# A bidirectional Mamba-2 block: gate columns of group 1 into the front, one PSUM ring of five banks in the scan, and three element-wise steps moved

## The chip, the cores and the metric

The kernel runs on one core of one Trainium2 chip. A core has TensorE (PE in the profile, its weight loads PEld), VectorE (DVE), ScalarE (ACT), GpSimd (POOL), SyncE (SP, which here only issues transfers), DMA queues, an on-chip memory called SBUF and the accumulators called PSUM, eight banks of 128 partitions by 512 fp32 numbers. Each engine runs its own instructions in the order in which they were written into its queue, and waits on semaphores for the others. The metric is the device time of one execution, in microseconds (us); lower is better.

## The reference

One layer, 1024 tokens, model width 1024, inner width 2048, 32 heads of 64 in 8 groups of 4, state size 128, chunks of 128 tokens. Everything is fp32.

```
u    = rmsnorm(x)
proj = u @ w_in                       # gate z (2048), x (2048), B and C (8 x 128 each), dt (2 x 32)
xBC  = silu(conv5(x, B, C))           # depthwise, centred
dt   = softplus(dt + bias);  a = -exp(a_log) * dt          # per direction and head
y    = x*d_skip + scan_forward(x*dt, a, B, C) + scan_backward(x*dt, a, B, C)
       # scan, per chunk: (C B^T * exp(segsum a)) x   +   exp(cumsum a) * C state_before
y    = y * silu(z);  y = y * rsqrt(mean over the 256 columns of a group of y^2 + eps)
out  = rmsnorm(x + (y * norm_w) @ w_out)
```

## The kernel before, in words

The program is written as loops over tiles. A scheduler, in which each instruction has a priority by the place where it is written and waits until its buffers are free, then decides the order on each engine. So the code's order and the number of buffers of each pool both move instructions.

**Front.** The eight token tiles of `x` are loaded, normalised, transposed by TensorE and cut into a high and a low fp32r half (`split`, L131 to L134: ScalarE copies, VectorE or GpSimd subtracts), so that three fast matmuls stand for one fp32 product. `z_products` (L137) multiplies one token chunk by a set of 256 gate columns: 8 slices by 3 matmuls, 24 a chunk, 192 a group of gate columns. Group 0's gate columns and the dt columns go this way in the front.

**Pairs.** Sixteen times (eight groups, B and C together and then x) a Strassen form of seven products of 12 matmuls with 512 columns each (`product`, L290; `pair_products`, L314), then the five-tap convolution (`conv`) and the way to DRAM. The weights' sums are made on GpSimd (L274) and split into `wh` and `wl` buffers. After the first pair's products are written, `decays` (L374) makes dt, the decays and their cumulative sums from the dt columns, and stores the rows of cumulative sums in DRAM (`rows_d`). The Strassen sum `t4` is made on GpSimd and split before the first pair.

**Scan.** For each group, `ssd_units` (L559) first builds the seven backward states (`state`, L551: GpSimd makes `xw`, one matmul; `update`, L539, two VectorE operations), and then goes over the eight chunks. One chunk needs, in this order: `mix` (L570), which loads two broadcasts `fb` of the cumulative sums, shifts one by four ScalarE operations (L580), selects by the triangle on VectorE (L582), takes exp on ScalarE (L585), multiplies by C B^T (`pcb`, L588) into `mt` (L590); the state terms `pyo` (L635) and the diagonal term `pyd` (L641) on TensorE; four VectorE operations into `y` (L644), eight ScalarE operations `yo` (L652) and two VectorE adds (L654); the product with the gate on GpSimd (L659); the square with its sum on ScalarE (L661), whose result goes into the unused half of the bank of `pyd`; the norm (L82, L85) and the scaling (L663); and one chunk later a transpose and four stores to `y_d` (`store`, L602).

PSUM in the scan: `pst` gives two banks, in which `pcb` and `pyd` take turns; `psh` gives two, for the states and `pyo`; `ps_ip` has the other four as two tiles of two banks, for gate columns and output units.

**Fills.** TensorE's gaps are filled with other work (`fills`, L769): the gate columns of groups 1 to 7 (`z_stream`, 192 matmuls each, the finished gate stored to DRAM by GpSimd's queue, L526), and then output units of the first half of the inner columns (`out_unit`, L707: 48 matmuls of 512 columns, then the sum with x into `h_d`). `AT` says at which steps of a group a piece is put in; `FIRST` says how many output units are asked for within the scan. What is left comes after the scan, and then the second half of the inner columns (half 1), whose weights `wo1` use the memory that the scan's buffers give up.

## Time and profile before

| | |
|---|---|
| median of 2 runs | 1131.33 us (1130.24 to 1132.42) |
| profiled execution | 1127.91 us, its span 1126.1 us |
| mean granted TensorE clock | 0.925 |
| PE, PEld busy | 977.5 us (87%), 816.6 us (73%) |
| DVE, ACT, POOL busy | 783.6 us (70%), 619.1 us (55%), 377.3 us (34%) |

Busy shares are averages over the whole program. A busy PE is an engine with a matmul under way, and since matmuls overlap and slow down with the clock, 87% is no measure of what is left to win. The stages have different limits, so the rows below are cut by stage: the front up to 153.9 us, the steady pairs to 448.7 us, a transition, the scan from its first diagonal matmul at 482.4 us, and the rest after 1020 us.

### The profile page before, as it was taken

Reading aid. Unit: us, or ns where it says so; the run is one execution under the profiler, and the core shown is the slowest. Engines: PE = TensorE matmul, PEld = TensorE weight load, DVE = VectorE, ACT = ScalarE, POOL = GpSimd, SP = SyncE. Lnnn points to the kernel's source line nnn. Section 1 sums busy time; section 2 is a strip of 40 time slices with the busy share of each in tenths; the row PEclk is TensorE's granted clock in tenths of the full one; section 3 lists DMA queues with packets and bytes.
Section 4 is the critical chain, followed back from the end, with each engine's and each line's share of the span. In section 5 each row is a group of like instructions: output and inputs, shape, how many; then the busy total and the mean of one; then the engine's idle time right before and its main releaser. Section 6 shows DMA issues by size and latency. Waiting matters only on the chain.

```text
span 1126.1 us, 16040 instructions
## 1 busy us (share of the span) xinstructions
PE 977.5 (87%) x5082; PEld 816.6 (73%) x5082; DVE 783.6 (70%) x1487; ACT 619.1 (55%) x1637; POOL 377.3 (34%) x424
## 2 busy tenths in 40 slices
PE   5784799999999999798999989897887897867997
PEld 4773578778778777688888978795665575645786
DVE  5557898788788788677877767867664775754433
ACT  5342455555555546467777757775663573753211
POOL 5349444353353340234333233424212323210000
PEclk9896899999999999899999998997588898968999
DMA  7221135244244227867767776777676766667431
GB/s 234 82 95 37 47 101 161 75 127 135 75 125 138 75 87 233 251 159 171 175 165 173 185 212 163 196 160 197 198 178 202 208 145 164 192 175 246 152 113 56
DMA packets 208212, 170.60 MB, mean 151 GB/s; under 512 B 78512, under 2 KB 177536, under 8 KB 207616
## 3 DMA queue, kind: packets, MB, share of 16 engines
...
HBM read 121.04 MB, written 48.50 MB: 151 GB/s over the span
## 4 chain that ended last, share of the span: by engine, by line
PE 52%; DVE 11%; issue 11%; DMA 9%; ACT 9%; POOL 7%; SPq 1%; POOLq 0%; DVEq 0%; ACTq 0%
PE x L295 12%; PE po L728 11%; PE BC L295 8%; DMA fb<-rows_d 6%; PE pz L146 5%; PE pyd L641 4%; POOL y L659 2%; PE pyo L635 2%; ACT fb L585 2%; ACT fb L580 2%; PE sf L556 1%; ACT yo L652 1%; DMA wo<-in_ssd_w_out_dram 1%; DMA wz<-in_ssd_w_in_dram 1%; PE pcb L588 1%
## 5 line engine op out<-in xcount | busy, mean ns | idle before, releaser
L652 ACT ACTIVATE yo<-pyo,ecs 128x64 f32<-128x64 f32 x448 | 104.2, 311 | 48.9 <-PE pyo L635 27.6
L659 POOL TENSOR_TENSOR y<-y,gt 128x256 f32<-128x256 f32 x64 | 55.3, 864 | 162.5 <-ACT fb L585 59.2
L580 ACT ACTIVATE fb<-fb,cfb 128x128 f32<-128x128 f32 x256 | 83.1, 394 | 48.2 <-DMA fb<-rows_d 43.6
L641 PE MATMUL pyd<-xb,mt 128*128 128x64 f32 x512 | 78.8, 305 | 26.9 <-ACT pyd L661 15.6
L641 PEld LDWEIGHTS pyd<-xb,mt 128*128 128x128 f32 x512 | 74.5, 221 | 36.5 <-ACT pyd L661 25.8
L585 ACT ACTIVATE fb<-fb,cfb 128x128 f32<-128x128 f32 x256 | 82.8, 395 | 20.4 <-DVE fb L582 19.9
L355 DVE SCALAR_TENSOR_TENSOR BC<-BC,prm,BC 128x1022 f32<-128x1022 f32 (+1 forms) x64 | 82.0, 1281 | 6.9 <-ACT BC L349 5.6
L644 DVE SCALAR_TENSOR_TENSOR y<-xb,coef,pyd 128x64 f32<-128x64 f32 x256 | 55.4, 276 | 44.2 <-PE pyd L641 44.0
L355 DVE SCALAR_TENSOR_TENSOR x<-x,prm,x 128x1022 f32<-128x1022 f32 (+1 forms) x64 | 81.8, 1278 | 1.2
L553 POOL TENSOR_TENSOR xwb<-xb,wdt 128x256 f32<-128x256 f32 x56 | 37.8, 684 | 95.0 <-DMA xb<-xb_d 48.7
L553 POOL TENSOR_TENSOR xwf<-xb,wdt 128x256 f32<-128x256 f32 x56 | 37.6, 674 | 88.7 <-PE sf L556 61.3
L582 DVE COPY_PREDICATED fb<-trif,fb 128x512 f32<-128x512 uint32 x64 | 49.8, 779 | 19.6 <-ACT fb L580 19.1
L590 DVE TENSOR_TENSOR mt<-fb,pcb 128x512 f32<-128x512 f32 x64 | 43.6, 683 | 21.9 <-ACT fb L585 21.1
L556 PE MATMUL sb<-xwb,xb 128*128 128x256 f32 x112 | 38.2, 439 | 19.0 <-POOL xwb L553 11.5
L728 PE MATMUL po<-wo1h,yh 128*128 128x512 f32 (+1 forms) x136 | 43.2, 389 | 8.6 <-ACT wo1h L682 7.9
L654 DVE TENSOR_TENSOR y<-y,yo 128x256 f32<-128x256 f32 x112 | 48.9, 437 | 2.4
L728 PE MATMUL po<-wo0h,yh 128*128 128x512 f32 x128 | 47.2, 448 | 3.5 <-ACT yh L132 2.6
L635 PE MATMUL pyo<-pf,ct 128*128 128x256 f32 x112 | 40.1, 443 | 8.7 <-ACT pf L544 4.9
L728 PE MATMUL po<-wo0l,yh 128*128 128x512 f32 x128 | 44.8, 429 | 1.9 <-DVE wo0l L683 1.9
L728 PE MATMUL po<-wo0h,yl 128*128 128x512 f32 x128 | 45.2, 425 | 0.2 <-DVE yl L133 0.2
L661 ACT ACTIVATE pyd<-y 128x256 f32<-128x256 f32 x64 | 24.7, 385 | 37.4 <-POOL y L659 36.9
L588 PE MATMUL pcb<-ct,bt 128*128 128x128 f32 x128 | 30.3, 326 | 16.8 <-ACT pyd L661 13.8
...
## 6 DMA issues: line engine op xcount, KB each, us to landing
fb<-rows_d SPq DMA_DIRECT2D x128, 256.0 KB, 4.7
...
y_d<-yt SPq DMA_DIRECT2D x256, 32.0 KB, 2.4
...
```

Of the source, the lines that this page charges most:

```text
L146: nc.tensor.matmul(pz[:, 0:m], a, b, start=at == 0, stop=at == 3 * NK - 1)
L295: nc.tensor.matmul(ps, a[:, k, :], b[:, k, :], start=fresh and n == 0, stop=n == 11, skip_group_check=True)
L355: nc.vector.scalar_tensor_tensor(out=acc[:, o], in0=ps[:, i], scalar=w(k), in1=acc[:, o], op0=ALU.mult, op1=ALU.add)
L553: nc.gpsimd.tensor_tensor(out=h4(xw), in0=h4(xb[:, 0:CW]), in1=bc4(wdt[:, d, c, g * HG:(g + 1) * HG], HD), op=ALU.mult)
L580: nc.scalar.activation(out=ef[:, h], in_=ef[:, h], func=AF.Identity, bias=cfb[:, 1, c, hsl(g, h)])
L585: nc.scalar.activation(out=ef[:, h], in_=ef[:, h], func=AF.Exp, bias=cfb[:, 0, c, hsl(g, h)])
L635: nc.tensor.matmul(pyo[:, d * CW:(d + 1) * CW], ct[:, tok], st, start=True, stop=True)
L641: nc.tensor.matmul(pyd[:, cs], mt[:, h, :], xb[:, cs], start=True, stop=True)
L644: nc.vector.scalar_tensor_tensor(out=y[:, cs], in0=xb[:, cs], scalar=coef[:, h:h + 1], in1=pyd[:, cs], op0=ALU.mult, op1=ALU.add)
L652: nc.scalar.activation(out=yo[:, cs], in_=pyo[:, d * CW + h * HD:d * CW + (h + 1) * HD], func=AF.Copy, scale=ecs[:, d, c, hsl(g, h)])
L659: nc.gpsimd.tensor_tensor(out=y, in0=y, in1=gt, op=ALU.mult)
L728: nc.tensor.matmul(pos[i], l_, r_[:, cols[i]], start=k == 0 and a == 0, stop=k == NO - 1 and a == 2)
```

## The change

Eight things are different.

1. PSUM. The two-bank pools now live only until the pairs end. In the scan there are three single banks for fills (`ps_z`) and one ring of five (`ps_h`), which `pcb`, `pyo`, `pyd` and the states share. After the scan, half 1 has five banks (`ps_o`). Gate columns are made two chunks at a time in one bank, and an output unit takes two single banks, so its sum with x becomes two operations.
2. The gate columns of group 1 (192 matmuls) are made in the front, and `decays` is written right behind them and ahead of the first pair.
3. Token tiles 2 and 6 of `x` are loaded into a tile of the weights' pool; the pool of high halves has 9 buffers, not 10.
4. Finished gates are stored through SP's queue in pieces of two chunks, not through GpSimd's in pieces of four.
5. The shift of the exponents is one GpSimd add on 128x512 instead of four ScalarE operations on 128x128.
6. The product of y and the gate is on VectorE, not on GpSimd.
7. The squares of y go to a tile in SBUF, not to the bank of `pyd`. `xw` has three buffers, not two.
8. `FIRST` is 7, `AT` has a 5 in place of a 6, the first four output weights are loaded while the last gate columns are made, and all eight weights of half 1 are asked for at once.

```diff
+    def z_group(g, w, bank, room, nxt=None):
+        for c0 in range(0, NC, 2):
+            gt = room(f"gate{g}_{c0}", (P, 2, CW))
+            pz = bank(f"pz{g}_{c0}").rearrange("p (i n) -> p i n", i=2)
+            for c in (c0, c0 + 1):
+                z_products(pz[:, c % 2], c, w, CW)
+                if c % 2:
+                    gate_of(gt, pz)
+                    nc.sync.dma_start(out=gate_d[g, :, c0:c0 + 2], in_=gt)
+                if c == NC // 2 and nxt is not None:
+                    nxt()
+                yield
...
-    WBUFS = {"h": 10, "l": 12}
+    WBUFS = {"h": 9, "l": 12}
...
-        xt = big(f"xt{t}")
+        if t == 2:
+            xts["pair"] = wpb.tile([P, 2, DM], F32, tag="raw", name="xt26")
+        xt = xts["pair"][:, t // 4] if t in (2, 6) else big(f"xt{t}")
...
+    for _ in z_group(1, load_z(1, wpb, (P, 4, 512)), pst, lambda n, sh: small("h", n, sh)):
+        pass
+    rows_v = decays()
...
-        if n == 0:
-            rows_v = decays()
...
-    ps_h = ctx.enter_context(tc.tile_pool(name="ps_h", bufs=2, space=PSUM))
+    ps_z = ctx.enter_context(tc.tile_pool(name="ps_z", bufs=3, space=PSUM))
+    ps_h = main.enter_context(tc.tile_pool(name="ps_h", bufs=5, space=PSUM))
...
-                        nc.gpsimd.dma_start(out=gate_d[g, :, c0:c0 + 4], in_=gt)
...
-        xw = sp.tile([P, CW], F32, tag="xw", name="xw" + name, bufs=2)
+        xw = sp.tile([P, CW], F32, tag="xw", name="xw" + name, bufs=3)
...
-            for h in range(HG):
-                nc.scalar.activation(out=ef[:, h], in_=ef[:, h], func=AF.Identity,
-                                     bias=cfb[:, 1, c, hsl(g, h)])
+            nc.gpsimd.tensor_tensor(out=ef, in0=ef, in1=bc4(cfb[:, 1, c, g * HG:(g + 1) * HG], P),
+                                    op=ALU.add)
...
-            pcb = pst(f"pcb{g}_{c}")
+            pcb = psh(f"pcb{g}_{c}")
...
-            pyd = pst(f"pyd{g}_{c}")
+            pyd = psh(f"pyd{g}_{c}")
...
-            nc.gpsimd.tensor_tensor(out=y, in0=y, in1=gt, op=ALU.mult)
+            nc.vector.tensor_tensor(out=y, in0=y, in1=gt, op=ALU.mult)
...
-            nc.scalar.activation(out=pyd[:, CW:2 * CW], in_=y, func=AF.Square, accum_out=ss)
+            junk = sp.tile([P, CW], F32, tag="junk", name=f"sq{g}_{c}", bufs=1)
+            nc.scalar.activation(out=junk, in_=y, func=AF.Square, accum_out=ss)
...
-            po = ps_ip.tile([P, DM], F32, tag="ip", name=f"po{half}{t}")
-            pos = [po[:, cs] for cs in cols]
+            pos = [obank(half)(f"po{half}{t}_{i}") for i in range(2)]
...
-            nc.vector.tensor_tensor(out=h, in0=po, in1=h, op=ALU.add)
+            for cs, pi in zip(cols, pos):
+                nc.vector.tensor_tensor(out=h[:, cs], in0=pi, in1=h[:, cs], op=ALU.add)
...
-    FIRST = 5
+    FIRST = 7
...
-        yield from z_stream(wz1)
-        for k in range(NO):
+        w = {2: wz2}
...
+        for g in range(2, NG):
+            yield from z_group(g, w.pop(g), psz, big, more(g))
+        for k in range(4, NO):
...
-    AT = (2, 6, 8, 9, 10, 11, 12, 13, 14, 15)
+    AT = (2, 5, 8, 9, 10, 11, 12, 13, 14, 15)
...
-        for _ in range(3):
+        for _ in range(NO):
```

The diff moves most instructions of the scan, and three places show how. The first is TensorE's order in group 4 of the scan, from the diagonal matmuls of chunk 1 on; `sf` is a forward state, `pz7` a gate fill of group 7. Before:

```order
L556 MATMUL sf4_1_7436<-xwf4_1_7434,xb4_1_7225 128x256
L588 MATMUL pcb4_2_7401<-ct4_7149,bt4_7148 128x128
L641 MATMUL pyd4_1_7412<-xb4_1_7225,mt4_1_7305 128x64 x4
L635 MATMUL pyo4_2_7501<-pf4_1_7438,ct4_7149 128x256
L635 MATMUL pyo4_2_7501<-pb4_2_7222,ct4_7149 128x256
L556 MATMUL sf4_2_7528<-xwf4_2_7526,xb4_2_7216 128x256
L146 MATMUL pz7_0_7643<-wz7_0h_7345,b11h_114 128x256
L146 MATMUL pz7_0_7643<-wz7_0l_7346,b11h_114 128x256
```

After the change, from chunk 0's state on:

```order
L565 MATMUL sf4_0_7572<-xwf4_0_7570,xb4_0_7507 128x256
L596 MATMUL pcb4_2_7623<-ct4_7376,bt4_7375 128x128
L643 MATMUL pyo4_1_7631<-pf4_0_7574,ct4_7376 128x256
L643 MATMUL pyo4_1_7631<-pb4_1_7458,ct4_7376 128x256
L649 MATMUL pyd4_1_7634<-xb4_1_7452,mt4_1_7546 128x64 x4
L565 MATMUL sf4_1_7658<-xwf4_1_7656,xb4_1_7452 128x256
L596 MATMUL pcb4_3_7715<-ct4_7376,bt4_7375 128x128
L643 MATMUL pyo4_2_7723<-pf4_1_7660,ct4_7376 128x256
L643 MATMUL pyo4_2_7723<-pb4_2_7449,ct4_7376 128x256
L649 MATMUL pyd4_2_7726<-xb4_2_7443,mt4_2_7625 128x64 x4
L565 MATMUL sf4_2_7750<-xwf4_2_7748,xb4_2_7443 128x256
```

What moved: `pcb` of chunk c+2 now stands ahead of `pyo` and `pyd` of chunk c+1, the forward state stands behind `pyd`, and no gate fill stands between these chunks; before, the next diagonal matmul in this order (chunk 2) stands behind 45 fill matmuls.

The second place is SP's queue in group 0 of the scan, chunks 2 to 4; `fb` are the broadcasts for `mix`, `gt` the gate that a chunk needs, `gate_d` is written by a store. Before:

```order
L442 DMA wz4_0_5315<-in_ssd_w_in_dram 128x4x256
L576 DMA fb0_2_3919<-rows_d_76 128x512 x2
L576 DMA fb0_3_4011<-rows_d_76 128x512 x2
L568 DMA xb1_7_4547<-xb_d_78 128x384
L626 DMA gt0_2_4009<-gate_d_80 128x256
L610 DMA y_d_77<-yt0_0_3979 32x8x32 x4
L576 DMA fb0_4_4106<-rows_d_76 128x512
L626 DMA gt0_3_4104<-gate_d_80 128x256
L576 DMA fb0_4_4106<-rows_d_76 128x512
```

After the change:

```order
L572 DMA ct1_4799<-bc_d_79 128x1024
L585 DMA fb0_2_4158<-rows_d_76 128x512 x2
L163 DMA gate_d_80<-gate2_0_3840 128x512
L163 DMA gate_d_80<-gate2_2_3893 128x512
L585 DMA fb0_3_4250<-rows_d_76 128x512 x2
L577 DMA xb1_7_4802<-xb_d_78 128x384
L634 DMA gt0_2_4248<-gate_d_80 128x256
L585 DMA fb0_4_4343<-rows_d_76 128x512
L163 DMA gate_d_80<-gate2_4_4005 128x512
L585 DMA fb0_4_4343<-rows_d_76 128x512
L577 DMA xb1_6_4804<-xb_d_78 128x384
L618 DMA y_d_77<-yt0_0_4216 32x8x32 x4
```

What moved: stores of gates now stand in SP's queue ahead of loads of `fb` and `gt` that the scan needs next. Between the first and the last chunk of the scan there are 24 of them; before, this queue had none and GpSimd's had all.

The third place is TensorE's order at the end of the scan, the last chunk of group 7; `po07` is output unit 7 of the first half, `po10` unit 0 of half 1. Before:

```order
L635 MATMUL pyo7_7_10187<-pf7_6_10168,ct7_9586 128x256
L588 MATMUL pcb7_7_10131<-ct7_9586,bt7_9585 128x128
L641 MATMUL pyd7_6_10142<-xb7_6_9591,mt7_6_10065 128x64 x4
L641 MATMUL pyd7_7_10189<-xb7_7_9589,mt7_7_10133 128x64 x4
L728 MATMUL po07_10389<-wo0h0_8298,yh070_10341 128x512 x2
L728 MATMUL po07_10389<-wo0l0_8299,yh070_10341 128x512 x2
```

After the change:

```order
L649 MATMUL pyd7_6_10226<-xb7_6_9692,mt7_6_10151 128x64 x4
L565 MATMUL sf7_6_10250<-xwf7_6_10248,xb7_6_9692 128x256
L643 MATMUL pyo7_7_10272<-pf7_6_10252,ct7_9687 128x256
L649 MATMUL pyd7_7_10274<-xb7_7_9690,mt7_7_10217 128x64 x4
L740 MATMUL po10_0_10428<-wo1h0_10385,yh100_10350 128x512
L740 MATMUL po10_1_10429<-wo1h0_10385,yh100_10350 128x512
```

What moved: the 48 matmuls of output unit 7 (six rows of two for each of four weights pairs) no longer stand between the last diagonal matmul and half 1; they are now within the scan.

## Rows read from the trace of the kernel before

**Rows 1.** Stretches: window, length, busy (instructions) PE, PEld, DVE, ACT, POOL; PEclk, DMA, GB/s.
```profile
0.00:74.90 74.90, 51.89 (x302) 47.77 (x302) 37.64 (x64) 31.11 (x59) 28.64 (x38) 0.93 0.47 150
74.90:153.90 79.00, 55.26 (x211) 41.38 (x212) 64.80 (x61) 32.43 (x52) 54.30 (x37) 0.81 0.19 54
153.90:448.70 294.80, 291.51 (x1330) 234.74 (x1328) 242.65 (x228) 166.00 (x253) 114.13 (x89) 1.00 0.39 120
482.40:1020.00 537.60, 463.65 (x2670) 395.57 (x2668) 374.07 (x1054) 350.24 (x1207) 168.20 (x244) 0.90 0.70 180
1020.00:1126.10 106.10, 91.12 (x408) 74.02 (x408) 42.16 (x55) 26.36 (x41) 4.38 (x8) 0.95 0.43 140
```

**Rows 2.** Gate matmuls, timeline of PE: start and length in us, engine, line.
```profile
554.37 0.28 PE L146 MATMUL pz<-wz_2h,b21h 128*128 128x256 f32 x1
555.67 0.28 PE L146 MATMUL pz<-wz_3h,b21l 128*128 128x256 f32 x1
```

**Rows 3.** The decays' first matmul, timeline of PE; idle before it in brackets.
```profile
126.76 0.77 PE L415 MATMUL pa<-dt,trif 128*128 128x256 f32 x1 [7.39 <-DVE dt L412]
```

**Rows 4.** Stretches of scan groups 1 and 5, and the sum over eight groups.
```profile
539.90:597.20 57.30, 54.16 (x395) 50.30 (x394) 45.90 (x132) 42.10 (x148) 23.04 (x33) 1.00 0.73 181
788.10:886.40 98.30, 78.33 (x287) 58.47 (x286) 60.46 (x146) 53.78 (x170) 21.67 (x31) 0.76 0.71 195
sum 537.60, PE 463.65 PEld 395.57 DVE 374.07 ACT 350.24 POOL 168.20; mean PE 57.96 PEld 49.45 DVE 46.76 ACT 43.78 POOL 21.03
```

**Rows 5.** Waits in the scan: engine, tile, line, releaser; total us, times, longest.
```profile
POOL xwf L553 <- PE sf L556: 61.3, 30, 4.7
ACT fb L580 <- DMA fb<-rows_d: 37.1, 24, 6.4
POOL gate_d L526 <- DVE gate L151: 17.3, 10, 5.3
PE pyd L641 <- ACT pyd L661: 15.6, 14, 4.1
PE pcb L588 <- ACT pyd L661: 13.8, 16, 3.2
```

**Rows 6.** Costliest groups of the page: busy us, mean ns, idle before.
```profile
L580 ACT ACTIVATE fb<-fb,cfb 128x128 f32<-128x128 f32 x256 | 83.1, 394 | 48.2 <-DMA fb<-rows_d 43.6
L659 POOL TENSOR_TENSOR y<-y,gt 128x256 f32<-128x256 f32 x64 | 55.3, 864 | 162.5 <-ACT fb L585 59.2
L654 DVE TENSOR_TENSOR y<-y,yo 128x256 f32<-128x256 f32 x112 | 48.9, 437 | 2.4
L661 ACT ACTIVATE pyd<-y 128x256 f32<-128x256 f32 x64 | 24.7, 385 | 37.4 <-POOL y L659 36.9
```

**Rows 7.** Line 663's instructions: min/median/max ns, first and last start.
```profile
L663 ACT ACTIVATE y<-y,y_7r x8: 507/509/510, 535.8 to 1010.7; 128x256 f32<-128x256 f32 x8
```

**Rows 8.** GpSimd and VectorE on 128x512 tiles, timeline of the front.
```profile
108.64 1.72 POOL L274 TENSOR_TENSOR wx0s<-wx0r 128x512 f32<-128x512 f32 x1
109.15 1.76 DVE L133 TENSOR_TENSOR wx0s2l<-wx0s,wx0s2h 128x512 fp32r<-128x512 f32 x1
...
126.53 0.68 DVE L133 TENSOR_TENSOR wBC1s2l<-wBC1s,wBC1s2h 128x512 fp32r<-128x512 f32 x1
...
141.77 1.29 POOL L274 TENSOR_TENSOR wx1s<-wx1r 128x512 f32<-128x512 f32 x1
```

**Rows 9.** From the last chunk to the first matmul of half 1, timeline.
```profile
1010.70 0.51 ACT L663 ACTIVATE y<-y,y_7r 128x256 f32<-128x256 f32 x1 [0.85 <-POOL y_7r L85]
...
1019.24 1.23 DVE L733 TENSOR_TENSOR h<-po,h 128x1024 f32<-128x1024 f32 x1 [4.82 <-PE po L728]
1020.38 0.43 DVE L606 STREAM_TRANSPOSE yt<-y 128x256 f32<-128x256 f32 x1
...
1024.15 2.19 ACT L682 ACTIVATE wo1h<-wo,prm 128x1024 fp32r<-128x1024 f32 x2 [6.34 <-DMA y_d<-yt]
...
1025.40 1.19 PE L728 MATMUL po<-wo1h,yh 128*128 128x512 f32 x2 [6.19 <-ACT wo1h L682]
```

More of the change, by code (lines that the diff above doesn't have):

```diff
@@ L56 @@
     dram = ctx.enter_context(tc.tile_pool(name="dram", bufs=1, space=bass.MemoryType.DRAM))
-    ps_ip = ctx.enter_context(tc.tile_pool(name="ps_ip", bufs=2, space=PSUM))
-    ps_g = ctx.enter_context(tc.tile_pool(name="ps_g", bufs=2, space=PSUM))
+    first = ExitStack()
+    ps_g = first.enter_context(tc.tile_pool(name="ps_g", bufs=2, space=PSUM))
+    ps_ip = first.enter_context(tc.tile_pool(name="ps_ip", bufs=2, space=PSUM))
     def pst(name):
@@ L94 @@
     dec = main.enter_context(tc.tile_pool(name="dec", bufs=1, side="right"))
-    first = ExitStack()
     ps_x = first.enter_context(tc.tile_pool(name="ps_x", bufs=1, space=PSUM))
@@ L199, in load_z0, with load_z @@
         return at
+    def load_z(g, pool, shape):
+        at = []
+        for i in range(2):
+            raw = pool.tile([P, 4, CW], F32, tag="raw", name=f"wz{g}_{i}", padded_shape=shape)
+            nc.sync.dma_start(out=raw, in_=w_in[:, 4 * i:4 * i + 4, g * CW:(g + 1) * CW])
+            for j in range(2):
+                hi, lo = (wtile(p, f"wz{g}_{2 * i + j}{p}", (P, 2, CW)) for p in "hl")
+                split(raw[:, 2 * j:2 * j + 2], hi, lo)
+                at += [(hi[:, n], lo[:, n]) for n in range(2)]
+        return at
     def to_cm(src, dst, tok, name):
@@ L705, in out_prep, with obank @@
         return h, yh, yl
+    ps_o = []
+    def obank(half):
+        return psz if half == 0 else lambda name: ps_o[0].tile([P, 512], F32, tag="o", name=name)
     def out_unit(half, t, wo, prep, nxt):
@@ L716, in out_unit @@
             steps = [(k, a, i) for i in range(3) for k, a in ka]
-            pos = [pst(f"po{i}")[:, 0:cs.stop - cs.start] for i, cs in enumerate(cols)]
+            pos = [obank(half)(f"po{i}")[:, 0:cs.stop - cs.start] for i, cs in enumerate(cols)]
         else:
-            po = ps_ip.tile([P, DM], F32, tag="ip", name=f"po{half}{t}")
-            pos = [po[:, cs] for cs in cols]
+            pos = [obank(half)(f"po{half}{t}_{i}") for i in range(2)]
             steps = [(k, a, i) for k, a in ka for i in range(2)]
@@ L732, in out_unit @@
         if half == 0:
-            nc.vector.tensor_tensor(out=h, in0=po, in1=h, op=ALU.add)
+            for cs, pi in zip(cols, pos):
+                nc.vector.tensor_tensor(out=h[:, cs], in0=pi, in1=h[:, cs], op=ALU.add)
             nc.sync.dma_start(out=h_d[tok, :], in_=h)
             return nprep
-        parts = list(zip(cols, pos)) if last else [(slice(0, DM), po)]
+        parts = list(zip(cols, pos))
         ss = ops.tile([P, 3], F32, tag="ss", name=f"oss{t}")
@@ L765, in finish, with more, do @@
                 return end.value
-    FIRST = 5
+    FIRST = 7
     wo1, preps = [], []
     def fills():
-        yield from z_stream(wz1)
-        for k in range(NO):
+        w = {2: wz2}
+        def more(g):
+            def do():
+                if g < NG - 1:
+                    w[g + 1] = load_z(g + 1, wp2, (P, 4, CW))
+                else:
+                    for k in range(4):
+                        if k % 2 == 0:
+                            tiles = wo_tiles(up, 0, k // 2)
+                        wo1.append(load_wo(tiles, 0, k))
+            return do
+        for g in range(2, NG):
+            yield from z_group(g, w.pop(g), psz, big, more(g))
+        for k in range(4, NO):
             if k % 2 == 0:
@@ L810 @@
     prep = preps[-1]
+    ps_o.append(ctx.enter_context(tc.tile_pool(name="ps_o", bufs=5, space=PSUM)))
     for t in range(NC):
```

30 lines of the change are left out of this document (5 added, 25 removed).

## The prediction

> **What bounds the kernel now.** I read the granted clock and engine shares first, then the span cut by stage [rows 1], then the scan by group [rows 4] and its waits [rows 5]; durations come from the page [rows 6] and single stretches of the timeline.
>
> The cut by stage shows where time can still be found. In the steady pairs TensorE is busy 291.5 of 294.8 us at clock 1.00: nothing is left there. Two stages are not like that. From 74.9 to 153.9 us TensorE is busy 55.3 of 79.0 us, so 23.7 us are idle, and its clock is 0.81, between the chip's two levels of 1.2 and 2.4 GHz. In the scan it is busy 463.7 of 537.6 us at 0.90, VectorE 374.1, ScalarE 350.2, GpSimd 168.2. No engine is full in the scan, so its length is set by waits of one engine for another.
>
> Which waits, the scan's list tells [rows 5]. The matmuls of `pyd` and `pcb` wait 15.6 and 13.8 us for the square of L661, since that square lies in the bank of `pyd` and both tiles share two banks: a chunk's bank comes free only after y, its adds, the gate product on GpSimd and the square. GpSimd waits 61.3 us for a forward state before it may overwrite one of two `xw`. ScalarE waits 37.1 us, once 6.4 us, for a broadcast `fb`. The groups differ: group 1 takes 57.3 us with TensorE busy 54.2 at clock 1.00, group 5 takes 98.3 us at 0.76 [rows 4].
>
> **The change part by part.** The sum is made against the profiled execution, 1127.91 us, which lies 3.4 us under the median of 1131.33; 3.4 us are added at the end.
>
> *x tiles.* More room lets two of eight loads start earlier. TensorE idles 23.0 of the first 74.9 us [rows 1], but the first loads and the splits hold it too, and no row parts them. Bounds 0 to -6 us (a quarter of that idle time); I take -3, the middle.
>
> *Gate columns of group 1 and the decays in the front.* Twelve gate matmuls start within 1.30 us [rows 2], so one takes 0.118 us and 192 take 22.7 us. They stand where TensorE now has 23.7 us idle, of which one wait of 7.39 us is the decays' first matmul, called for by VectorE after pair 0 has begun [rows 3]. In the change the decays' VectorE work runs under the 192 matmuls, and pair 0 starts later by these but without that wait. What stays uncovered is the wait for `t4`, whose sums run on GpSimd (busy 54.3 of 79.0 us there). If it all fits, the cost is 0; if nothing does, +22.7. Since the room is just the size of the work, but the clock of 0.81 leaves some more, I take 0, and keep -3 to +23. Leaving the scan, the same 192 matmuls give TensorE 22.7 us there, counted below.
>
> *Nine buffers of high halves.* A pair keeps seven live, so two are left for the next pair instead of three. The stage has 3.3 us of TensorE idle time now. Taken as 0; bounds 0 to +8 (0.6 us in each of some 14 pairs).
>
> *The shift on GpSimd.* ScalarE loses 256 operations, 83.1 us, nearly all inside the scan's stretch [rows 6]. GpSimd gains 64 adds on 128x512; such an add took it 1.29 us alone and 1.72 beside VectorE [rows 8], 83 to 110 us in all. It loses 55.3 us of gate products [rows 6]. GpSimd in the scan: 168.2 - 55.3 + 83 to 110 = 196 to 223 us, below half of the stage, so it is not the bound by its sum. The latency of a chunk's shift, four times 394 ns = 1.58 us before, is about the same.
>
> *The gate product on VectorE.* The nearest row is the add of the same shape, 437 ns [rows 6]: 64 x 0.437 = 28.0 us more on VectorE. A chunk's chain loses 0.43 us (864 - 437 ns) and one crossing between engines.
>
> *Squares to SBUF.* A ScalarE pass on the same 128x256 from SBUF to SBUF takes 508 ns [rows 7], to PSUM 385 [rows 6]: 64 x 0.12 = 7.9 us more on ScalarE, which has 350.2 - 83 + 8 = 275 us of work left in the scan. Hidden: ScalarE then has over 200 us free, and nobody waits for the bank any more. The Trainium skill, "ScalarE: Activation LUTs", section "Step-by-step: what each stage is for", says that ScalarE writes to PSUM faster than to SBUF; both rows here agree, and by it this step is a loss, which is worth it only if the bank was the wait.
>
> *Five banks in a ring.* A chunk takes four banks (`pcb`, `pyo`, `pyd`, `sf`). With five, a bank is asked for again five takes later, and it comes free after y, after `yo` or after the state update, not after the square. The 29.4 us of TensorE's waits for L661 go, and so does most of the 61.3 us of GpSimd, which was not on TensorE's path by itself (third `xw`).
>
> *What the scan then takes.* Two floors. VectorE: 374.1 + 28.0 = 402. To it comes contention: VectorE operations from SBUF are stretched while GpSimd adds (1.76 us against 0.68 [rows 8], 1.08 us more). GpSimd's adds in the scan rise by 28 to 55 us net; the adds of L654 (48.9 us) and the gate product (28) are a fifth of VectorE's 402 us, and with the selects of L582 I take 30% of its time to be operations from SBUF, so I put 12 us: 414, or 51.8 us a group. TensorE: group 1 has 257 gate matmuls in its order, 30.3 of 54.2 us, which leaves 24 us of a group's own matmuls; 8 x 24 and the fills make 400: six groups of gate columns at 22.7 us, less 14 that run before the scan, and the 384 matmuls of eight output units at 91.12/408 = 0.223 us [rows 1], 208 in all. VectorE is the larger. What a group takes above VectorE's work now is 57.3 - 45.9 = 11.4 us in an undisturbed group [rows 4], 7.7 if the 29.4 us of bank waits, 3.7 a group, come off in full. So 8 x (51.8 + 7.7 to 11.4) = 476 to 505, and I take 488, **-50** us. It comes mostly from the slow groups 4 to 7, where TensorE's clock fell after waits. Bounds: -95 (all waits gone but 3 us a group: 8 x 54.8 = 438, rounded up for the dearer transition) and the rivals below.
>
> *Gate stores on SP.* 14 issues leave GpSimd's queue, where one had waited 1.7 us on average for its data (17.3 us over 10 [rows 5]); 24 come onto SP's in the scan, each half as large. Behind a waiting store stand the loads of `fb` and `gt`. A load is issued a chunk ahead, so at 1.7 us each I take 0; at worst see the second rival.
>
> *End of the scan.* Now, after the last scaling ends at 1011.2, TensorE does output unit 7, VectorE adds it at 1019.24 for 1.23 us, and only then comes the last transpose at 1020.38; its stores land, `wo1h` starts at 1024.15 and half 1 at 1025.40 [rows 9]. With unit 7 inside the scan the transpose can follow the scaling: 1011.3 + 0.4, then the same 3.3 and 1.25 us, so about 1016.3 instead of 1025.4: **-9**. Bounds -10 to -4. The 48 matmuls, 10.7 us, are in the fills above.
>
> *Output units in single banks, weights of half 1 all at once:* the same matmuls and one more VectorE start each; 0, bounds -3 to +3, hidden behind 48 matmuls a unit.
>
> Sum: 1127.9 - 3 + 0 + 0 - 50 - 9 = 1065.9, and with 3.4 **1069 us**.
>
> **The rivals.** A measurement of this kernel can tell about 2%, 23 us, from no change: faster means under 1109, slower over 1154.
>
> *VectorE held up by GpSimd.* Each of the 64 large adds might meet a VectorE operation from SBUF and stretch it by the full 1.08 us: 69 us, VectorE 374 + 28 + 69 = 471, 58.9 a group, and with 7.7 to 11.4 on top 533 to 562 us of scan, middle 548: 1127.9 - 12 + 10 + 3.4 = 1129. For it: the doubled row, and that the change puts the gate product, an operation with two SBUF operands, beside the adds. Against it: most of VectorE's work in the scan reads PSUM or one operand. The Trainium skill, "SBUF — State Buffer", section "Who interferes with whom", has the rule: VectorE's second port pair is GpSimd's, under an exclusive lock. The stretched row agrees; by that rule part 5 of the change speaks against part 6. The chance of this rival is 13%.
>
> *Slower: SP's head of line.* A gate store that waits for its gate holds `fb` and `gt` behind it; `fb` is what starts the next `mix`. If each of the 24 costs the scan the longest wait that GpSimd's stores had, 5.3 us [rows 5], that is 127 us: 1069 + 127 = 1196. It decides once a store costs more than (1154 - 1069)/24 = 3.5 us. For it: `fb` already makes ScalarE wait up to 6.4 us, and two buffers give little lead. Against: mean waits were 1.7 us. Chance 10%.
>
> *The front does not hide group 1.* The 192 matmuls lengthen the front by 22.7 us: 1092. For it: the wait for `t4` is on GpSimd and may move behind them. Chance 12%.
>
> *The ring does not free.* Five takes back from the next `pyd` stands `pyo`, freed by eight ScalarE operations of `yo`; if that comes as late as the square did, the chunk's pace stays and the scan wins only the 22.7 us that left it, less the 10.7 of unit 7: 1127.9 - 3 - 12 - 9 + 3.4 = 1107. Chance 8%.
>
> **The numbers.** The forecast has 57% (range 1035 to 1105). The range must hold 80%: forecast, front and ring cases, and a part of the first rival: 1030 to 1118. Left out are SP's case, most of the first rival, and a little below. Faster: nearly all of the forecast, the front's 12% and half of the ring's 8%, about 72%; same: 18%; slower: 10%.
>
> **What would show it.** In the profile after: no wait of `pyd` or `pcb` for the square, and none in its place; the scan's stretch at 475 to 505 us with VectorE at 400 to 420; groups 4 to 7 near 60 us and a clock near 1.00; GpSimd's adds at 1.3 to 1.7 us; pair 1 starting at about 154 us; half 1 within 10 us of the last diagonal matmul. Wrong would be: VectorE's two-operand operations at twice their time, `fb` waits above 37 us with a store ahead of them on SP, a new wait of TensorE for `yo`, or pair 1 at 175.

## The result, and the profile after

The change made the kernel slower: 1160.11 us (1159.33 to 1160.89) against 1131.33, ratio 1.0254 [1.0203, 1.0306]. The forecast was 1069, the range 1030 to 1118.

The cut by stage of the kernel after, with the columns of [rows 1], cut where pair 2 is first copied (pairs counted from 0; the prediction's signs call it pair 1) and where the scan's first diagonal matmul starts:

```profile
0.00:74.90 74.90, 51.23 (x306) 46.91 (x306) 37.98 (x65) 31.66 (x60) 29.81 (x38) 0.93 0.40 136
74.90:163.10 88.20, 75.54 (x400) 63.71 (x400) 59.96 (x68) 36.02 (x58) 49.72 (x36) 0.90 0.32 91
163.10:457.00 293.90, 280.77 (x1279) 225.32 (x1278) 236.95 (x214) 157.63 (x240) 126.37 (x89) 1.00 0.36 106
...
505.30:1046.00 540.70, 443.21 (x2485) 382.76 (x2483) 388.39 (x1128) 274.34 (x959) 167.47 (x226) 0.86 0.66 175
1046.00:1159.20 113.20, 91.38 (x408) 74.57 (x408) 44.81 (x72) 30.09 (x60) 4.95 (x9) 0.89 0.41 132
```

The front takes 163.1 us instead of 153.9. TensorE does fill its idle time there (75.5 of 88.2 us), but the stage is longer by 9.2. In the scan VectorE is at 388 us, near the forecast 402, ScalarE at 274, where 275 was forecast. The engines' sums are near the forecast or below it; the stage is not.

A table tells where the time lies, worked out from the start of each chunk's first diagonal matmul and from the first copies of pairs 2 and 15. "Chunks" are the seven steps within each group, "transitions" the seven steps from a group's last diagonal matmul to the next group's first.

| us | front | pairs 2 to 15 | to the scan | chunks | transitions | rest |
|---|---|---|---|---|---|---|
| before | 153.9 | 276.1 | 52.5 | 400.6 | 122.1 | 120.9 |
| after | 163.1 | 287.7 | 54.5 | 355.5 | 178.4 | 120.0 |
| difference | +9.2 | +11.6 | +2.0 | -45.1 | +56.3 | -0.9 |

The chunks did become shorter, by 45 us, 28.5 of them in group 5 alone, whose seven steps fell from 67.5 to 39.0 us (in the other groups they took 44.8 to 50.3 before). Nearly everything else went the other way. Groups 4 to 6, which were to come near 60 us at a clock near 1.00, take 80.0, 70.0 and 71.4 us at 0.78, 0.91 and 0.85; before, they took 64.4, 98.3 and 71.5. The waits of the scan after, as in [rows 5]:

```profile
POOL xwf L562 <- PE sf L565: 80.3, 26, 6.4
POOL fb L588 <- DMA fb<-rows_d: 52.3, 21, 5.1
PE pyd L649 <- DVE mt L598: 44.0, 17, 18.3
DVE fb L590 <- POOL fb L588: 43.8, 30, 5.7
```

No wait of `pyd` or `pcb` for the square is in the list: this step did what it said. In its place `pyd` waits 44.0 us for `mt`, once 18.3, and `mt` for a chain that begins with GpSimd waiting for `fb`. The costliest groups, as in [rows 6]:

```profile
L588 POOL TENSOR_TENSOR fb<-fb,cfb 128x512 f32<-128x512 f32 x61 | 65.4, 1072 | 77.0 <-DMA fb<-rows_d 52.3 <-ACT fb L593 10.1 <-issue 4.3
L662 DVE TENSOR_TENSOR y<-y,yo 128x256 f32<-128x256 f32 x112 | 50.3, 449 | 2.4 <-ACT yo L660 1.6
L667 DVE TENSOR_TENSOR y<-y,gt 128x256 f32<-128x256 f32 x63 | 27.4, 434 | 0.4
L670 ACT ACTIVATE sq<-y 128x256 f32<-128x256 f32 x63 | 26.6, 422 | 25.7 <-DVE y L667 25.4
```

The shift takes GpSimd 1.07 us, less than the 1.29 taken from [rows 8]. VectorE's operations from SBUF take 434 and 449 ns on average, against 437 in [rows 6]. These means hide that few of them meet the shift. Of the 112 adds ten overlap it, and these take 697 ns on average; the 91 that meet no GpSimd instruction over 0.3 us take 414, none more than 426. One that does, by the timeline (start, length, engine, line, operation):

```profile
788.99 1.04 POOL L588 TENSOR_TENSOR fb<-fb,cfb 128x512 f32<-128x512 f32 x1 [2.01 <-DMA fb<-rows_d]
789.32 0.99 DVE L662 TENSOR_TENSOR y<-y,yo 128x256 f32<-128x256 f32 x1
```

With four products of the gate that overlap it (664 ns against 417), this adds up to about 4 us in the whole scan.

The growth of the transitions is uneven: 5.2, 18.5, 20.7 and 11.0 us in the transitions from groups 0, 1, 3 and 4, and 1.2 us or less in the three others. The one that grew most is shown here. First its stretch before (group 3 to 4) and after, columns as in [rows 1]:

```profile
713.00:723.70 10.70, 9.51 (x66) 8.45 (x67) 8.77 (x26) 5.65 (x18) 5.69 (x9) 1.00 0.63 149
```

```profile
746.50:777.90 31.40, 10.19 (x56) 8.44 (x55) 17.06 (x34) 9.77 (x21) 10.13 (x14) 0.69 0.69 192
```

TensorE is busy 9.5 of 10.7 us before and 10.2 of 31.4 after, at a clock of 0.69. The timeline of the transition before, around the last diagonal matmul of group 3 (start, length, engine, line, operation; SPq is SP's queue):

```profile
710.61 0.86 SPq L576 DMA_DIRECT2D fb<-rows_d  x2
712.99 1.07 PE L641 MATMUL pyd<-xb,mt 128*128 128x64 f32 x8 [0.30 <-DVE y_6m L82]
713.83 1.80 SPq L610 DMA_DIRECT2D y_d<-yt  x4
715.74 0.40 SPq L568 DMA_DIRECT2D xb<-xb_d  x1
716.25 0.36 SPq L626 DMA_DIRECT2D gt<-gate_d  x1
```

The last `xb` of the next group is issued 2.8 us after that matmul; the next group's first `fb` was issued 2.4 us before it. The same place after the change (last diagonal matmul at 746.54):

```profile
756.36 1.80 SPq L618 DMA_DIRECT2D y_d<-yt  x4
758.20 0.92 SPq L688 DMA_DIRECT2D wo<-in_ssd_w_out_dram  x2
759.97 1.83 SPq L618 DMA_DIRECT2D y_d<-yt  x4
762.00 2.41 ACT L691 ACTIVATE wo0h<-wo,prm 128x1024 fp32r<-128x1024 f32 x2 [1.46 <-DMA wo<-in_ssd_w_out_dram]
764.49 1.61 SPq L688 DMA_DIRECT2D wo<-in_ssd_w_out_dram  x2
766.16 0.42 SPq L577 DMA_DIRECT2D xb<-xb_d  x1
766.63 0.90 SPq L585 DMA_DIRECT2D fb<-rows_d  x2
...
771.32 2.73 POOL L562 TENSOR_TENSOR xwf<-xb,wdt 128x256 f32<-128x256 f32 x3 [14.88 <-DMA xb<-xb_d]
774.02 1.03 POOL L588 TENSOR_TENSOR fb<-fb,cfb 128x512 f32<-128x512 f32 x1
...
777.90 0.69 PE L649 MATMUL pyd<-xb,mt 128*128 128x64 f32 x2 [18.33 <-DVE mt L598]
```

SP issues stores of y, two output weights, stores of y again, and then waits until a raw weight has been read (ScalarE starts on it at 762.00) before it can issue the next two at 764.49. Only behind these come `xb` at 766.16 and `fb` at 766.63, 20 us after the last diagonal matmul. GpSimd idles 14.9 us for `xb`, and the first diagonal matmul of group 4 waits 18.3 us. By the start times of the loads, the mean over the seven transitions is: last `xb` 5.4 us after the last diagonal matmul before and 13.3 after, first `fb` 4.2 and 13.7, first diagonal matmul 17.4 and 25.5. On average the transition grew by what the loads came later.

The end of the scan, timeline, as in [rows 9]; first the last diagonal matmul before, then the kernel after:

```profile
1005.16 1.94 PE L641 MATMUL pyd<-xb,mt 128*128 128x64 f32 x8 [4.40 <-DVE y_6m L82]
```

```profile
1039.19 1.97 PE L649 MATMUL pyd<-xb,mt 128*128 128x64 f32 x8 [0.59 <-DVE mt L598]
...
1044.32 0.45 DVE L614 STREAM_TRANSPOSE yt<-y 128x256 f32<-128x256 f32 x1 [0.55 <-DMA y_d<-yt]
...
1049.66 0.45 DVE L614 STREAM_TRANSPOSE yt<-y 128x256 f32<-128x256 f32 x1 [0.32 <-DMA y_d<-yt]
1050.07 0.51 ACT L672 ACTIVATE y<-y,y_7r 128x256 f32<-128x256 f32 x1 [1.18 <-POOL y_7r L86]
...
1053.25 0.45 DVE L614 STREAM_TRANSPOSE yt<-y 128x256 f32<-128x256 f32 x1 [0.38 <-DMA y_d<-yt]
1053.72 1.79 SPq L618 DMA_DIRECT2D y_d<-yt  x4
...
1058.80 2.19 ACT L691 ACTIVATE wo1h<-wo,prm 128x1024 fp32r<-128x1024 f32 x2 [1.28 <-DMA y_d<-yt]
1060.05 1.62 PE L740 MATMUL po<-wo1h,yh 128*128 128x512 f32 x3 [18.90 <-ACT wo1h L691]
```

Output unit 7 is gone from this place, and yet half 1 starts 20.9 us after the last diagonal matmul starts, as before (1005.16 to 1025.40, 20.2 us). Four transposes into the one buffer `yt` (at 1039.38 and the three shown) stand behind it, each after the stores of the one before; before there were three (at 1006.00, 1010.07 and, behind unit 7, 1020.38). No run gave `yt` a second buffer, so that this backlog is the wait is read from the timeline alone.

### The profile page after: what moved, and what is told of

Its sections match the earlier page's. It is cut to its first block, busy times and chain, and to the rows that moved or that the text cites. A ratio compares the mean times of both kernels' runs of the same rounds, so it can differ in the third digit from the quotient of the medians.

```text
span 1159.2 us, 15961 instructions
## 1 busy us (share of the span) xinstructions
PE 977.0 (84%) x5082; PEld 822.8 (71%) x5082; DVE 803.1 (69%) x1587; ACT 548.6 (47%) x1409; POOL 389.6 (34%) x410
## 4 chain that ended last, share of the span: by engine, by line
PE 52%; DVE 13%; DMA 12%; issue 8%; ACT 6%; POOL 6%; SPq 3%; POOLq 0%; DVEq 0%; ACTq 0%
PE po L740 12%; PE pz L146 11%; PE x L323 9%; PE BC L323 8%; DMA fb<-rows_d 6%; PE pyd L649 4%; PE pyo L643 2%; DVE x L383 2%; POOL fb L588 2%; PE sf L565 2%; DMA xb<-xb_d 2%; DMA wo<-in_ssd_w_out_dram 2%; SPq L618 1%; ACT fb L593 1%; DMA y_d<-yt 1%
## 5 line engine op out<-in xcount | busy, mean ns | idle before, releaser
L649 PEld LDWEIGHTS pyd<-xb,mt 128*128 128x128 f32 x512 | 77.0, 225 | 63.0 <-DVE mt L598 58.0
L593 ACT ACTIVATE fb<-fb,cfb 128x128 f32<-128x128 f32 x256 | 83.0, 392 | 77.1 <-DVE fb L590 70.6
L588 POOL TENSOR_TENSOR fb<-fb,cfb 128x512 f32<-128x512 f32 x64 | 68.5, 1071 | 88.8 <-DMA fb<-rows_d 64.2
L562 POOL TENSOR_TENSOR xwf<-xb,wdt 128x256 f32<-128x256 f32 x56 | 36.7, 665 | 105.0 <-PE sf L565 80.3
L565 PE MATMUL sb<-xwb,xb 128*128 128x256 f32 x112 | 40.6, 480 | 25.1 <-POOL xwb L562 17.4
L662 DVE TENSOR_TENSOR y<-y,yo 128x256 f32<-128x256 f32 x112 | 50.3, 449 | 2.4 <-ACT yo L660 1.6
L565 PEld LDWEIGHTS sb<-xwb,xb 128*128 128x128 f32 x112 | 22.4, 231 | 35.6 <-POOL xwb L562 29.8
L740 PE MATMUL po<-wo1l,yh 128*128 128x512 f32 (+1 forms) x136 | 43.3, 386 | 0.7 <-DVE wo1l L692 0.7
L151 DVE SCALAR_TENSOR_TENSOR gate<-gate,pz 128x512 f32<-128x512 f32 x32 | 21.8, 682 | 31.7 <-ACT gate L150 31.7
```

What stands on the lines that cost most here:

```text
L562: nc.gpsimd.tensor_tensor(out=h4(xw), in0=h4(xb[:, 0:CW]), in1=bc4(wdt[:, d, c, g * HG:(g + 1) * HG], HD), op=ALU.mult)
L565: nc.tensor.matmul(ps[:, 0:CW], xb[:, CW:CW + P], xw, start=True, stop=True)
L588: nc.gpsimd.tensor_tensor(out=ef, in0=ef, in1=bc4(cfb[:, 1, c, g * HG:(g + 1) * HG], P), op=ALU.add)
L593: nc.scalar.activation(out=ef[:, h], in_=ef[:, h], func=AF.Exp, bias=cfb[:, 0, c, hsl(g, h)])
L649: nc.tensor.matmul(pyd[:, cs], mt[:, h, :], xb[:, cs], start=True, stop=True)
L740: nc.tensor.matmul(pos[i], l_, r_[:, cols[i]], start=k == 0 and a == 0, stop=k == NO - 1 and a == 2)
```

## The experiments

Runs on "the change" start from the kernel after, those on "before" from the kernel before; `comb1` and what follows it are described where they come. All times are medians, ratios are to the kernel before on the same chip.

**One buffer less** (`b_h9`, on before).

```diff
-    WBUFS = {"h": 10, "l": 12}
+    WBUFS = {"h": 9, "l": 12}
```

> The kernel before with 9 instead of 10 buffers for high halves, nothing else. In the profile of the change the steady pairs (from the first copy of pair 2 to that of pair 15) take 287.7 us against 276.0. Theory A, the lost buffer costs this: the stretch becomes 285 to 290 us here and the total 1140 to 1146. Rival B, the cost comes from the decays and the gate columns of group 1 being written ahead of the pairs: stretch 276 to 278, total 1130 to 1134.

1138.05 us, 1.0084 [1.0057, 1.0111]; pairs 290.0 us. The buffer alone costs the pairs 13.9 us, and the rival is out: with ten buffers and the gate columns in the front the pairs take 275.8 us (`c_z1_front`, below). TensorE's one long idle time in a group's pairs is the same in the change and here:

```profile
215.80 1.06 PE L397 MATMUL x0t_1p<-ident,x 128*128 128x128 f32 x8 [1.86 <-DVE x L387]
```

```profile
206.87 1.66 PE L369 MATMUL x0t_1p<-ident,x 128*128 128x128 f32 x8 [1.85 <-DVE x L359]
```

With nine buffers the transposes of x stand in TensorE's order 1.9 us before VectorE has their operand, once in each group; in the kernel before, this wait is 0.8 us once and else under 0.4. The rest of the run also shows how far the split of the scan can move by itself: its chunks are 384.6 and its transitions 142.1, 16 us less and 20 more than before, though no line of the scan differs.

**Single parts of the change undone** (`a_shift_act`: ScalarE's shift of before; `a_gate_pool`: `nc.gpsimd.dma_start` for the gate; `a_sched`: part 8 undone but for the weights of half 1; `a_z1_scan`: part 2 undone).

> The change with the exponents' shift back on ScalarE. Theory Q: in the change the diagonal matmuls wait 44 us for mt, whose chain runs through GpSimd's queue, where the shift stands behind the tiny power operations that wait for the norm; back on ScalarE the scan (533.9 us from the first to the last diagonal matmul) loses 20 to 40 us, total 1120 to 1140. Rival S: the chain is late because SP's queue issues fb late (gate stores, y stores and output weights ahead of it); then total 1155 to 1165, and the wait of ScalarE for fb comes back.

> The change with the gate stores back on GpSimd's queue (pieces of two chunks). Rival S (SP's head of line by gate stores): the scan loses 20 us or more, total under 1140. Theory Q: GpSimd's queue gets 24 more waits, total 1158 to 1170.

> The change with FIRST 5, AT with its 6, and all eight output weights of half 0 loaded after the last gate columns, as before. Theory W: the 18.3 us wait at the start of group 4 of the scan comes from two output weights ahead of xb and fb in SP's queue, waiting for a raw buffer; it goes, and the part from group 3's last diagonal matmul to group 5's first (111.3 us) falls to about 95; total 1140 to 1150. If the schedule only moves this wait to the next group: 1155 to 1165. The 48 matmuls of unit 7 return to the end of the scan in part: +5 to +9 there.

> The change with the gate columns of group 1 made in the scan again and the decays behind pair 0 again; the nine buffers stay. Front (to the first copy of pair 2) 163.1 us in the change, 153.9 before. Theory F: the 192 matmuls were hidden only in part, so the front falls to about 154 (-9) and the scan's fills grow by 22.7 us; if the scan has idle time for them (TensorE idles 93 of 534 us there) the scan grows by 5 or less and the total is 1150 to 1157; if the scan is paced by its fills, it grows by 15 to 23 and the total is 1165 to 1173.

| on the change | us | ratio | front | chunks | transitions | rest |
|---|---|---|---|---|---|---|
| shift on ScalarE | 1148.50 | 1.0188 [1.0135, 1.0241] | 162.6 | 370.5 | 158.1 | 115.2 |
| gate stores by GpSimd | 1147.02 | 1.0164 [1.0117, 1.0210] | 166.7 | 346.8 | 167.9 | 121.4 |
| old schedule | 1161.22 | 1.0296 [1.0238, 1.0354] | 163.7 | 370.7 | 157.7 | 124.3 |
| group 1 in the scan | 1154.19 | 1.0217 [1.0168, 1.0266] | 152.9 | 364.7 | 167.2 | 117.6 |

By medians the shift and the gate stores cost 12 and 13 us, by ratios 7 and 10, between what their two theories had said. All four intervals overlap with that of the change, so these runs alone are weak, and three of the parts are put to `comb1` below. The schedule is a wash: the 31.4 us transition falls to 21.1, but the weights now come inside group 4, whose chunks rise from 54.8 to 70.1. With group 1 back in the scan the front is 10.2 us shorter and the scan, which has 22.7 us more of TensorE's work, is not longer (532.0 against 533.9): TensorE's work does not set the scan's time.

**The square's place and the ring alone** (`b_sq_yo`, on before; `ring_only`, whose PSUM pools are the change's).

```diff
-            nc.scalar.activation(out=pyd[:, CW:2 * CW], in_=y, func=AF.Square, accum_out=ss)
+            nc.scalar.activation(out=yo, in_=y, func=AF.Square, accum_out=ss)
```

> The kernel before with one operand changed: the squares go to the dead tile yo in SBUF, not to the bank of pyd. Theory R (the step of the prediction): the 29 us of waits of pyd and pcb for the square go, and the scan (522.7 us from first to last diagonal matmul) falls by 15 to 30 us; total 1100 to 1115. Theory C (the wait only changes its name, since a chunk is paced by the chain fb, shift, select, exp, mt): same within 5 us, 1126 to 1136, with pyd waiting for mt instead.

> The kernel before with the PSUM layout of the change (three banks for fills, a ring of five for the scan, half 1 in five, gates stored in pieces of two chunks through GpSimd's queue) and the squares in SBUF; ten buffers, shift on ScalarE, gate product on GpSimd, FIRST 5, xw 2, group 1 in the scan. Theory R: scan below 500 us, total 1095 to 1110. Theory C: 1125 to 1138.

1123.61 us, 0.9962 [0.9934, 0.9990], and 1115.71 us, 0.9879 [0.9840, 0.9917]; chunks and transitions 370.4 and 143.2, 368.7 and 140.6. Both theories were too sure. Waits of the scan of `b_sq_yo`:

```profile
DVE y L644 <- PE pyd L641: 21.9, 33, 1.9
PE pyd L641 <- DVE pcb L594: 19.1, 17, 5.7
PE pyd L641 <- DVE mt L590: 13.5, 3, 5.6
```

The waits for the square (29.4 us in [rows 5]) are gone. In their place stand 32.6 us for C B^T's diagonal and `mt`, of which 6.5 were there before and 5.6 lie ahead of the first diagonal matmul: about 20 us are new, and the scan is 9.0 us shorter (513.7 against 522.7).

**A version that is faster** (`comb1`): `ring_only`, but with the gate product on VectorE and what it lacked of part 8 (it already asks for all weights of half 1 at once). That is the change without parts 2, 3, 4 (pieces of two chunks stay, on GpSimd's queue) and 5, the squares in the dead tile `yo`, and two `xw`.

> As ring_only, but with the gate product on VectorE and the schedule of the change (FIRST 7, AT 5, four output weights early, weights of half 1 at once). Theory R: 9 us below ring_only at the end of the scan. Theory C: the output weights ahead of xb and fb cost 10 to 20 us at the start of a group, as in the change; total not below ring_only.

1103.11 us, 0.9759 [0.9710, 0.9809]. Three of the parts left out were then put back alone (`c_gate_sp`, `c_shift_pool`, `c_z1_front`), and the gate product put back on GpSimd (`c_ygt_pool`). Nine buffers were run alone only on the kernel before; the third `xw`, the squares' own tile and the tiles of x were not run alone.

> comb1 (1103 us) with the exponents' shift on GpSimd, nothing else. Theory Q (the shift in GpSimd's in-order queue is late, the mt chain with it): scan 8 to 15 us longer, total 1110 to 1120, ScalarE waiting for the select (L588) more than the 32.6 us of comb1 at that place. Rival: on a kernel without gate stores in SP's queue the shift costs nothing, total 1098 to 1108, and the cost in the change was SP's.

> comb1 with the gate stores in SP's queue, nothing else. Theory S (SP's head of line): 28 stores hold loads of fb, xb and gt behind them, scan 10 to 20 us longer, total 1113 to 1123. Rival: the 52.6 us that GpSimd waits for gates in comb1 weigh as much, total 1095 to 1108.

> comb1 with the gate product on GpSimd. If the gate product on VectorE is what makes comb1 12 us faster than ring_only: 1112 to 1118. If the schedule (FIRST 7, weights early) does: 1100 to 1106.

> comb1 with the gate columns of group 1 and the decays ahead of the pairs, ten buffers kept. Theory F: the front grows by 7 to 10 us (its idle time is no room, since t4 and the weights' sums come later too), the pairs stay at 276, the scan gives back at most 5 though its fills lose 22.7 us, since waits pace it; total 1105 to 1113. Rival: with ten buffers the front hides it and the scan gains 10 to 20, total 1083 to 1095.

| on comb1 | us | ratio | front | chunks | transitions | rest |
|---|---|---|---|---|---|---|
| comb1 | 1103.11 | 0.9759 [0.9710, 0.9809] | 155.8 | 357.0 | 138.9 | 116.5 |
| shift on GpSimd | 1140.63 | 1.0078 [1.0048, 1.0109] | 156.0 | 366.0 | 158.2 | 122.2 |
| gate stores by SP | 1128.60 | 0.9964 [0.9939, 0.9988] | 154.6 | 370.0 | 149.3 | 118.7 |
| group 1 in the front | 1128.82 | 0.9983 [0.9959, 1.0008] | 167.6 | 362.3 | 147.4 | 116.6 |
| gate product on GpSimd | 1115.24 | 0.9858 [0.9810, 0.9907] | 153.0 | 367.8 | 141.1 | 116.2 |

The chips of the runs differ, so the costs are taken from the ratios, times 1131 us: 36 us for the shift, 23 for the gate stores, 25 for group 1, each with intervals apart from that of `comb1` and more than was expected. The gate product on VectorE is worth 11 us, and the rest of part 8 nothing: `c_ygt_pool` differs from `ring_only` by it alone, 1115.24 and 1115.71. The waits of `comb1` and of the run with GpSimd's shift:

```profile
ACT fb L586 <- DMA fb<-rows_d: 38.7, 25, 7.0
DVE fb L588 <- ACT fb L586: 32.6, 26, 8.9
PE pyd L647 <- DVE mt L596: 23.2, 16, 6.0
ACT fb L591 <- DVE fb L588: 6.8, 10, 1.3
```

```profile
POOL fb L585 <- DMA fb<-rows_d: 60.0, 26, 4.2
DVE fb L587 <- POOL fb L585: 58.4, 35, 8.7
ACT fb L590 <- DVE fb L587: 50.2, 30, 9.2
PE pyd L646 <- DVE mt L595: 31.1, 21, 6.2
```

With the shift on ScalarE, exp waits 6.8 us for the select and the select 32.6 for the shift; with it on GpSimd these are 50.2 and 58.4. Yet the shift does not come late: from the issue of a chunk's second `fb` load to the end of its select the mean of the 64 chunks is 8.6 us in `comb1` and 8.1 with GpSimd's shift. What comes later is y and the next group. From a chunk's first diagonal matmul to the last of its stores it is 17.7 us instead of 15.1, and the last `xb` of the next group is issued 10.8 us after the last diagonal matmul instead of 6.7. What ties this to the shift is not shown.

**Taking loads out of SP's queue, and opening the loop over `fb`.** `a_fb_act` and `c_fb_act` issue `fb` by `nc.scalar.dma_start`, `a_xb_pool` and `c_ef4_xb` issue `xb` by `nc.gpsimd.dma_start`. `a_ef4` and `c_ef4`:

```diff
-            fb = sp.tile([P, 2, HG, P], F32, tag="fb", name=f"fb{g}_{c}")
+            fb = [sp.tile([P, HG, P], F32, tag=f"fb{d}", name=f"fb{d}{g}_{c}", bufs=(2, 4)[d])
+                  for d in range(2)]
...
-            mt = sp.tile([P, HG, P], F32, tag="mt", name=f"mt{g}_{c}")
+            mt = ef
```

> The change with the loads of fb issued through ScalarE's queue, nothing else. In the change the first fb of a group is issued 21.2 us after its buffer is free (11.8 before), in chunks 2 to 7 after 0 to 3 us. Theory S (SP's in-order queue holds that load behind gate, y and xb transfers): the lag falls below 14 us, the scan (533.9 us) by 25 to 50, total 1110 to 1135. Theory Q (GpSimd's shift is what is late): lag and scan as they were, total 1150 to 1165.

> The change with the loads of xb issued through GpSimd's queue. In the change the last xb of a group is issued 13.3 us after the last diagonal matmul of the group before (5.4 before) and the first diagonal matmul follows 25.5 us after it (17.4 before). Theory S (transfers in SP's order hold xb and fb): xb comes earlier and SP's queue is shorter, transitions (178.4 us) fall by 20 or more, total 1130 to 1145. Theory Q (GpSimd's queue is the late one): 64 more issues there make it worse, 1160 to 1180.

> The change with fb cut in its two halves, two buffers for the forward rows and four for the backward rows, in which mt is then made in place (the same SBUF). Theory L (a loop of load, shift, select, exp, mt over two buffers sets the pace of a chunk at 6 to 7 us, and the start of a group waits for it): chunks fall to about 6 us, the groups' transitions by 5 us or more, scan below 500, total below 1125. If the loop is no bound: 1150 to 1165.

> comb1 with the loads of fb through ScalarE's queue. Theory S: without gate stores in SP's queue there is less to pass, so a gain of 0 to 12 us, 1090 to 1103; if ScalarE's own waits hold the loads as SP did, 1103 to 1115.

> comb1 with the same cut of fb. Theory L: scan 496 to about 465 to 480 us, where VectorE's work (about 50 us a group) is next, total 1072 to 1090. If the loop is no bound: 1098 to 1108.

> c_ef4 (1096 us), whose chunks take 324 us and whose transitions take 160, with xb loaded through GpSimd's queue. Theory S: transitions fall by 10 to 25, total 1072 to 1088. If GpSimd's own waits (gates, norms) hold xb as SP's did: 1092 to 1110.

| | us | ratio | chunks | transitions | first fb, last xb after the last diagonal matmul |
|---|---|---|---|---|---|
| the change | 1160.11 | 1.0254 [1.0203, 1.0306] | 355.5 | 178.4 | 13.7, 13.3 |
| its fb by ScalarE | 1146.37 | 1.0144 [1.0113, 1.0175] | 370.2 | 139.7 | -5.9, 12.5 |
| its xb by GpSimd | 1163.92 | 1.0307 [1.0268, 1.0345] | 387.3 | 143.2 | 6.4, 4.8 |
| its fb in 2 and 4 buffers | 1166.44 | 1.0316 [1.0292, 1.0339] | 354.7 | 180.0 | 12.4, 13.2 |
| comb1, fb by ScalarE | 1135.97 | 1.0040 [1.0018, 1.0062] | 400.1 | 120.4 | 1.2, 2.5 |
| **comb1, fb in 2 and 4 buffers** | **1095.99** | **0.9698 [0.9672, 0.9724]** | 324.1 | 160.5 | 8.6, 12.3 |
| the same, xb by GpSimd | 1098.91 | 0.9750 [0.9693, 0.9807] | 333.1 | 142.8 | -9.6, 10.8 |

In the change, taking either load out of SP's queue brings it earlier and cuts the transitions by 35 to 39 us, to 139.7 and 143.2. `b_h9`, `b_sq_yo`, `ring_only`, `comb1` and `c_ygt_pool` lie there too (138.9 to 143.2), with neither gate stores on SP nor the shift on GpSimd. So about 20 of the 56 us need neither of these parts, and the rest goes when one of the loads leaves SP's queue. But with `fb` the chunks give 15 us back, with `xb` 32: the first leaves the scan 24 us shorter and the kernel 12 us by the ratios, the second 3 us shorter and the kernel no faster. Why the chunks give it back is not shown. On `comb1`, without gate stores on SP, moving `fb` is a plain loss (32 us by the ratios): within a group ScalarE issues the first load 3.5 us after its buffer is free, SP 2.7, and the second 2.6 us behind it, SP 1.0. The loop over two `fb` buffers is a bound of the chunks in `comb1` (357.0 to 324.1, of which the transitions take 22 us back) and none in the change. The fastest version is `c_ef4`, ahead of both kernels; its interval overlaps a little with that of `comb1`. Its scan against that of `comb1`, columns as in [rows 1]:

```profile
490.40:986.30 495.90, 438.85 (x2666) 382.37 (x2665) 383.19 (x1121) 343.27 (x1203) 120.75 (x191) 0.94 0.71 187
```

```profile
489.50:974.10 484.60, 427.31 (x2620) 372.64 (x2619) 374.91 (x1117) 337.50 (x1193) 123.02 (x191) 0.93 0.75 189
```

## Why the prediction was wrong

The step that failed is **"What the scan then takes"**: VectorE's work per group plus 7.7 to 11.4 us. It took what a group needs above VectorE's work from an undisturbed group of the kernel before and let only the bank waits fall off it. That remainder was never the one of all groups: over the eight it was 20.4 us before ((537.6 - 374.07)/8), and after the change it is 19.0 ((540.7 - 388.39)/8), with VectorE's work at 48.5 instead of 51.8. So the slow groups did not come down to the undisturbed one, and the scan took 540.7 us, not 488. Of the 95 us between the forecast of the profiled execution (1065.9) and the measured 1160.9, 61 lie in the scan (+11 us from its first to its last diagonal matmul, against -50), 12 each in the front and the pairs, 8 at the end and 2 ahead of the scan.

Much of the remainder lies at the change of groups, where the next group's first chunk needs `xb` and `fb`, and these stand in SP's one queue. The change moved this queue: on average the loads came 8 to 9.5 us later, a transition grew by 8.1 us, and 56 us went there while the chunks gained 45.

Point by point:

- *Bank waits, ring and squares:* mechanism right, size too large. The waits went; ring and squares are worth 14 us by the ratio of `ring_only`, not 29.4, and other waits of `pyd` stand in their place. The rival of a ring that does not free did not show: in the change the matmuls of `pyd` and `pyo` wait 1.8 us for `yo`. GpSimd's wait before `xw`, most of which was to go, rose from 61.3 to 80.3 us with three buffers.
- *Gate product on VectorE:* right, 11 us on `comb1`. VectorE's sum came to 388 us, 14 under the 402 and 26 under the 414 with contention.
- *Gate stores on SP:* taken as 0, cost 23 us on `comb1` and 10 to 13 in the change (there not clear of noise). The slower rival named this queue and put the deciding price at 3.5 us a store; by the undone stores it is 0.5 (13/24). Nor was it the store's own wait: in the scan SP waited 13.7 us before gate stores, 0.6 each, and 92.4 before stores of y. So the rival had the right queue and not the right reason: ahead of `xb` and `fb` the timeline shows stores of y and output weights, which the prediction did not count.
- *The shift on GpSimd:* costed as hidden because GpSimd's sum was low. It cost 36 us on `comb1` and 7 to 12 in the change (there not clear of noise), though GpSimd is busy only 167 us of the scan and the shift itself is not late. The rival of a held-up VectorE was right in kind and far too large: its operations are stretched where they meet the shift, but only 14 do, for 4 us and not 69, and the 12 us of contention in the sum were too many as well. The Trainium skill's exclusive lock ("SBUF — State Buffer", "Who interferes with whom") agrees with these rows.
- *Group 1 in the front:* the rival of an uncovered front was right in part: +9.2 us in the change, 10.2 by undoing it. "Leaving the scan, the same 192 matmuls give TensorE 22.7 us there" was wrong: on the change the scan gave nothing back (533.9 us, 532.0 with group 1 in it), on `comb1` it became 14 us longer.
- *Nine buffers:* bounded at +8, measured +11.6 in the change and +13.9 alone. It was taken as 0 for TensorE's 3.3 us of idle time in the pairs, which says nothing of an order that changes.
- *End of the scan:* -9 forecast, -0.9 came. Without the 48 matmuls there, stores of y through one buffer are the wait, by the timeline. With the old schedule the rest is 4 us longer (124.3 against 120.0), so a part of the gain was there.
- *x tiles:* no run shows an effect; kernels with the old tiles and group 1 in the scan have fronts of 152.8 to 156.0 us, and so has the change with group 1 in the scan.

The costs found singly on `comb1` (36, 23, 25, and 14 of the pairs) add up to 98 us, the change lies 56 above `comb1`. They overlap, and how is open. Open is also by what way the shift on GpSimd costs this much, since it is short and not late; a changed order on GpSimd, where norms and `xw` stand in the same queue, is a guess that no run tried alone.
